# Later and fewer early weight sums, gate rows at a set place, output projection by token halves of two steps at a time

## The chip, the cores and the metric

The kernel runs on one core of a Trainium2 chip. The metric is the device time of one execution in microseconds; the time of a version is the median of several executions. The core's engines work side by side, each through its own instructions in order: TensorE (PE: matmuls and transposes), VectorE (DVE), ScalarE (ACT), GpSimd (POOL), and SyncE (SP), which here issues nearly all transfers between HBM and the on-chip memory.

## The reference

One layer of a residual block over 512 tokens of width 2048, all in float32, with 16 heads of width 128 in two groups: 8 stick-breaking heads and 8 forgetting heads, then a multilayer perceptron of hidden width 8192.

```python
h = rmsnorm(x, g_attn[l])
proj = jnp.einsum('bsd,de->bse', h, w_in[l])     # qa ka va | qf kf vf | f
...
z = z + c[:, :, i * Q_BLOCK:end, None] - c[:, :, None, :end]   # forgetting heads, c = cumsum(log_f)
p = jax.nn.softmax(jnp.where(causal, z, -jnp.inf), axis=-1)
...
a = jnp.where(causal, jnp.exp(log_beta + rest), 0.0)           # stick-breaking heads
...
x = x + concat(headnorm(oa), headnorm(ob)) @ W_out
x = x + relu(RMSNorm(x) @ W_up)^2 @ W_down
y = RMSNorm(x)
```

## The kernel before

**Numbers.** Every float32 operand is split into a high part (a cast by ACT, line 63) and a low part (a subtraction by DVE, line 64). A product is three matmuls, high x high, low x high and high x low (`mm3`, lines 95 to 98). So each block of weights costs a load on SP, a cast on ACT, a subtraction on DVE and then matmuls. Buffers for the parts come in a ring of three (`hi_lo`).

**Stages, in us of the profiled execution.** 0 to 50: x is transposed, and the first values and the gate columns f are projected (tiles accv, accm). 50 to 636: for each of 16 heads q and k are projected (`project_q`, tile accq, two steps of 24 matmuls each), the values in four groups, and the heads are worked off. 636 to 825: output projection (`out_product`, tile acco) in four column blocks n, residual and transposes. 825 to 1460: up projection. 1460 to 2050: down projection (tile accd), then the last rows.

**The attention's order on PE.** From line 529 on PE's order is written by hand: `in_turn` yields after small groups of projection matmuls, each with its time at 0.2267 us a matmul, and a table puts the heads' parts between them. Head i is at `HEAD_AT[i]`: scores there, transposes of the weights 22 us later (TURN), the product with the values 6 us after that (WEIGH, tile o), and `SUM` us after that ssq, the sum of squares for the head's norm (lines 315, 316). One PSUM bank (tag "o") holds cps, cT, ck, o and ssq in turn. DVE, ACT and SP are ordered by the scheduler.

**The gate rows.** The cumulative log gates are formed by matmuls with a triangle (cps, line 463), brought to a high and a low part on DVE (cq, chl, lines 466 to 469), transposed by four PE transposes (cT, line 472) and copied (ckT, line 474). For each forgetting head a matmul with a selector, ck (line 346), spreads one row. Before, cps and cT stand outside of the hand-written order.

**Early sums.** The up projection works unit by unit, 32 units of 256 columns, each as a 2 x 2 block product by seven products instead of eight (Strassen in Winograd's form). Three of the seven need a sum of weight blocks: t1 = b12 - b11, t3 = b22 - b12 and t2 = b22 - t1. They are formed ahead of time, during the attention, by `up_sums` (lines 156 to 164): three loads of 512 KB, three subtractions of 128x1024 on DVE, and one store to the DRAM tile td. `drip` (line 169) sets the place: behind the n-th low part of a projection step, DVE's subtractions of unit number 32 n / 62 follow. In the up projection `Unit` (line 625) loads t1, t2, t3 from td, and b21 and b22 from w_up. Products run in the order 1, 4 (of the unit before), 5, 6, 3 (of the unit before), 2, 7; product 6 takes t2. Its PSUM tiles are psa, psb and psc.

**Output projection.** `out_product` (line 228) takes two heads' rows per step: a load of w_out, its split, the split of two mixed rows (four sets of u tiles), then for each of four token blocks t two `mm3`, six matmuls. Each token block has a PSUM bank of the pool acc, which the values used before: `take_v` (line 244) splits them out of the banks into vh and vl. For n == 0 the generator runs inside the hand-written order, between the last heads' parts.

Of the kernel before, what the change touches and what calls it, by code (L numbers as in the profile page):

```python
# [14 lines left out]
P = 128  # L15
# [4 lines left out]
NH = 8  # L20
# [8 lines left out]
HEAD_AT = [26, 60, 96, 134, 163, 195, 230, 265, 294, 327, 362, 395.5, 419, 444, 468, 495]  # L29
TURN, WEIGH, SUM, VALUES_END = 22, 6, 5, 503  # L30
# [8 lines left out]
def block_kernel(ctx, tc, x, g_attn, w_in, b_f, g_out_sb, g_out_fox, w_out, g_mlp, w_up, w_down, g_final, y):  # L39
# [116 lines left out]
    def up_sums():  # L156
        r = load_sums(0)
        for u in range(NU):
            b11, b12, b22 = (r[:, j] for j in range(3))
            now, r = r, load_sums(u + 1) if u + 1 < NU else None  # L160
            dve.tensor_tensor(b11, b12, b11, op=ALU.subtract)
            dve.tensor_tensor(b12, b22, b12, op=ALU.subtract)
            dve.tensor_tensor(b22, b22, b11, op=ALU.subtract)
            yield sp.dma_start(td[u], now)
# [4 lines left out]
    def drip(ins):  # L169

        drops[0] += 1
        while drops[1] < min(NU, NU * drops[0] // 62):
            drops[1] += 1
            with tc.issue_after(ins.ins):
                next(sums)


    with (
# [49 lines left out]
        def out_product(n, mixed):  # L228
            ps = [acc.tile([P, NT], F32, tag="acc", name="acco") for _ in range(TB)]
            for k0 in range(0, 2 * NH, 2):  # L230
# [3 lines left out]
                for i in range(2):  # L234
                    ms.append(u_tile((k0 + i) % 4))
                    split(*ms[i], mixed[k0 // NH][:, (k0 + i) % NH, :])
                for t in range(TB):
                    ts = slice(t * P, (t + 1) * P)
                    for i in range(2):
                        mm3(ps[t], ms[i][0][:, ts], ms[i][1][:, ts], *w[i], k0 + i == 0, k0 + i == 2 * NH - 1)  # L240
                    yield 6 * 0.2267
# [200 lines left out]
        with tc.tile_pool(name="attp", bufs=1, space=PSUM) as atp:  # L442
# [27 lines left out]
            cT = atp.tile([P, NT], F32, tag="o", name="cT")  # L470
            for t in range(TB):
                pe.transpose(cT[:, t * P:(t + 1) * P], chl[:, t, :], ident)
            ckT = at.tile([P, NT], F32R, name="ckT")
            act.copy(ckT, cT)
# [37 lines left out]
            steps = []  # L512
# [9 lines left out]
            def run(i, part):  # L522
                with tc.high_priority():
                    if part < 0:
# [100 lines left out]
    class Unit:  # L625
        def __init__(self, u):
# [19 lines left out]
            for t_, j in ((t1, 0), (t2, 2), (t3, 1)):  # L646
                sp.dma_start(t_, td[u][:, j])
# [4 lines left out]
        def product(self, p):  # L652
# [5 lines left out]
            hi, lo = (w.rearrange("p (a b) -> p a b", b=P) for w in hi_lo(2 * NT))  # L658
            split(hi, lo, self.b[p])
# [317 lines left out]
```

## Time and profile before

| | us |
|---|---|
| three runs, median | 2084.97 (2084.62 to 2085.84) |
| profiled execution, whole | 2085.26 |
| its span | 2083.5 |
| PE busy in the span | 2055.4 |
| mean granted clock of PE | 0.997 |

The profile is one execution. Its page gives busy times, a chain of waits and groups of instructions; the trace behind it answers questions on single instructions. A row of a timeline reads: start, duration (both us), engine, line, operation, output<-inputs, shapes, and in brackets the idle time before it and what ended that. A row "L64 ... wl<-wraw,wh" is a low part of weights. A matmul's duration includes its way through the array; the distance between starts tells the pace. In a windows row, after the bounds, stand length, busy time and count of PE, weight loads, DVE, ACT and POOL, then the granted clock of PE (1.00 is full), the share of the DMA engines' time, and GB/s.

### The profile page before, as it was taken

To read this page: it belongs to the slowest core of one execution; us is meant where nothing else is said; L and a number is where in the kernel's file an instruction comes from. 1 tells how busy PE (TensorE), PEld (TensorE's weight loads), DVE (VectorE), ACT (ScalarE), POOL (GpSimd) and SP (SyncE) were. 2 spreads that over 40 slices of the span, in tenths; PEclk is the share of its full clock that TensorE was granted. 3 is DMA by queue.
4 is the path that set the end of the run, shared out by engine and by line. 5 is a ranking of instruction groups with operands and counts; after the bars stand their busy time and mean duration, and the time that the engine had idled before them with its cause. 6 is when DMAs were issued, how large, how long until landed. Compare 5 with 4: busy or idle time off the path is not lost.

```text
span 2083.5 us, 26844 instructions
## 1 busy us (share of the span) xinstructions
PE 2055.4 (99%) x10292; PEld 1747.1 (84%) x10292; DVE 1606.7 (77%) x1827; ACT 1070.1 (51%) x1426; POOL 57.1 (3%) x77
## 2 busy tenths in 40 slices
PE   9999999999999999999999999999999999999998
PEld 8788888888888888888888888888888888888886
DVE  6657848858776666788788788788789989888886
ACT  6344434445555555666666666666644444443433
POOL 0000000000110000000000000000000000000003
PEclk9999999999999999999999999999999999999999
DMA  7967957969972444677777777778856764764732
GB/s 238 342 203 245 329 175 242 334 181 293 329 251 74 158 133 151 203 263 255 250 266 258 245 265 257 246 265 295 304 200 229 254 236 164 270 231 139 271 113 81
DMA packets 361185, 481.06 MB, mean 231 GB/s; under 512 B 11952, under 2 KB 255712, under 8 KB 350944
## 3 DMA queue, kind: packets, MB, share of 16 engines
q1 hardware_dynamic: 360096, 477.21, 68.4%
q10 hardware_dynamic: 960, 2.13, 0.3%
q8 instruction: 81, 1.33, 0.2%
q14 instruction: 48, 0.39, 0.1%
HBM read 359.76 MB, written 119.54 MB: 230 GB/s over the span
## 4 chain that ended last, share of the span: by engine, by line
PE 90%; DMA 4%; DVE 4%; ACT 1%; issue 1%; SPq 0%; POOL 0%; DVEq 0%; ACTq 0%; POOLq 0%
PE psa L665 11%; PE accd L96 8%; PE accd L97 8%; PE accd L98 8%; PE psa L667 6%; PE psc L665 6%; PE accq L96 4%; PE accq L98 4%; PE accq L97 4%; PE psc L667 3%; PE psb L665 3%; PE acco L96 3%; PE acco L98 3%; PE acco L97 3%; PE accv L96 3%; PE accv L97 2%
## 5 line engine op out<-in xcount | busy, mean ns | idle before, releaser
L63 ACT CAST wh<-wraw 128x1024 fp32r<-128x1024 f32 (+2 forms) x133 | 135.4, 1019 | 201.0 <-PE accq L97 109.6
L63 ACT CAST wh<-wd 128x1024 fp32r<-128x1024 f32 (+1 forms) x136 | 135.1, 1000 | 182.3 <-PE accd L98 120.5
L64 DVE TENSOR_TENSOR wl<-wu,wh 128x1024 fp32r<-128x1024 f32 x166 | 201.6, 1219 | 32.0 <-ACT wh L63 18.3
L64 DVE TENSOR_TENSOR wl<-wraw,wh 128x1024 fp32r<-128x1024 f32 (+2 forms) x133 | 158.3, 1191 | 86.6 <-ACT wh L63 84.0
L63 ACT CAST wh<-wu 128x1024 fp32r<-128x1024 f32 x166 | 173.3, 1049 | 72.2 <-PE psc L665 20.5
L96 PE MATMUL accq<-hH,wh 128*128 128x512 f32 x512 | 201.8, 394 | 0.0
L98 PE MATMUL accq<-hH,wl 128*128 128x512 f32 x512 | 200.4, 392 | 0.0
L97 PE MATMUL accq<-hL,wh 128*128 128x512 f32 x512 | 200.1, 391 | 0.0
L64 DVE TENSOR_TENSOR wl<-wd,wh 128x1024 fp32r<-128x1024 f32 (+1 forms) x136 | 155.4, 1152 | 42.3 <-ACT wh L63 42.1
L96 PE MATMUL accd<-wh,uf 128*128 128x512 f32 x436 | 169.7, 389 | 0.9 <-issue 0.9
L97 PE MATMUL accd<-wl,uf 128*128 128x512 f32 x436 | 169.6, 389 | 0.0
L98 PE MATMUL accd<-wh,uf 128*128 128x512 f32 x436 | 169.6, 389 | 0.0
L63 ACT CAST wx<-wd 128x1024 fp32r<-128x1024 f32 (+1 forms) x88 | 87.6, 1000 | 122.1 <-PE accd L98 79.5
L64 DVE TENSOR_TENSOR wx<-wd,wx 128x1024 fp32r<-128x1024 f32 (+1 forms) x88 | 100.7, 1152 | 22.4 <-ACT wx L63 22.3
L98 PEld LDWEIGHTS accq<-hH,wl 128*128 128x128 f32 x512 | 96.4, 188 | 20.4
L97 PEld LDWEIGHTS accq<-hL,wh 128*128 128x128 f32 x512 | 96.7, 189 | 19.5
L96 PEld LDWEIGHTS accq<-hH,wh 128*128 128x128 f32 x512 | 96.6, 189 | 19.0
L96 PE MATMUL accd<-wx,uf 128*128 128x512 f32 x284 | 110.4, 389 | 1.2 <-ACT m L764 1.2
L97 PE MATMUL accd<-wx,uf 128*128 128x512 f32 x284 | 110.5, 389 | 0.0
L98 PE MATMUL accd<-wx,uf 128*128 128x512 f32 x284 | 110.5, 389 | 0.0
L766 DVE TENSOR_TENSOR m<-m,accd 128x1024 f32<-128x1024 f32 x84 | 102.0, 1214 | 10.8 <-PE accd L98 10.7
L665 PE MATMUL psa<-fl,wh 128*128 128x512 f32 x388 | 106.8, 391 | 1.8 <-DVE fl L64 1.8
(285 smaller groups left out, 4857.6 us busy)
## 6 DMA issues: line engine op xcount, KB each, us to landing
ufd<-st SPq DMA_DIRECT2D x98, 512.0 KB, 5.2
sums<-in_w_up_dram SPq DMA_DIRECT2D x96, 512.0 KB, 6.2
td<-sums SPq DMA_DIRECT2D x32, 1536.0 KB, 7.5
wd<-in_w_down_dram SPq DMA_DIRECT2D x48, 1024.0 KB, 6.5
wu<-td SPq DMA_DIRECT2D x95, 512.0 KB, 5.0
wraw<-in_w_in_dram SPq DMA_DIRECT2D x84, 512.0 KB, 5.8
uf<-ufd SPq DMA_DIRECT2D x42, 1024.0 KB, 6.7
wu<-in_w_up_dram SPq DMA_DIRECT2D x32, 1024.0 KB, 7.6
```

What stands on the lines that cost most here:

```text
L63: ins = casts[0] = act.copy(hi, src)
L64: lows[0] = dve.tensor_tensor(lo, src, hi.bitcast(F32), op=ALU.subtract)
L96: pe.matmul(out, sh, mh, start=first, stop=False, skip_group_check=True)
L97: pe.matmul(out, sh, ml, start=False, stop=False, skip_group_check=True)
L98: pe.matmul(out, sl, mh, start=False, stop=last, skip_group_check=True)
L665: pe.matmul(ps, hi[:, a, :], both, start=a == 0 and p in (1, 2, 5), stop=False, skip_group_check=True)
L667: pe.matmul(ps[:, :2 * P], lo[:, a, :], F[p][a // 4][:, a % 4, 0, :], start=False, stop=a == KC // 2 - 1, skip_group_check=True)
L766: dve.tensor_tensor(M[p][:, :, db, :], M[p][:, :, db, :], ps, op=ALU.add)
```

## The change

Five edits:

- `HEAD_AT[0]` goes from 26 to 33 and `HEAD_AT[1]` from 60 to 62; `SUM` from 5 to 7.
- The drip begins later: unit number 32 (n - 4) / 58 instead of 32 n / 62.
- For odd units the third sum t2 isn't formed early, and only two of three blocks are stored to and read from td. In its place `Unit.product` forms b22 - t1 ahead of the split of product 6, on DVE.
- The transposes of the gate rows and their copy become `turn_bias`, which the hand-written order calls at `HEAD_AT[0] - 9`, 24 us.
- In `out_product` with n == 0 the first two steps are held and then done together: twelve matmuls per token block instead of six, twice.

```diff
--- before.py
+++ after.py
@@ -26,8 +26,8 @@
 O1 = 6 * WSB
 NU = DFF // P // 2
 
-HEAD_AT = [26, 60, 96, 134, 163, 195, 230, 265, 294, 327, 362, 395.5, 419, 444, 468, 495]
-TURN, WEIGH, SUM, VALUES_END = 22, 6, 5, 503
+HEAD_AT = [33, 62, 96, 134, 163, 195, 230, 265, 294, 327, 362, 395.5, 419, 444, 468, 495]
+TURN, WEIGH, SUM, VALUES_END = 22, 6, 7, 503
 
 
 
@@ -160,8 +160,10 @@
             now, r = r, load_sums(u + 1) if u + 1 < NU else None
             dve.tensor_tensor(b11, b12, b11, op=ALU.subtract)
             dve.tensor_tensor(b12, b22, b12, op=ALU.subtract)
-            dve.tensor_tensor(b22, b22, b11, op=ALU.subtract)
-            yield sp.dma_start(td[u], now)
+            if u % 2 == 0:
+                dve.tensor_tensor(b22, b22, b11, op=ALU.subtract)
+            n = 2 if u % 2 else 3
+            yield sp.dma_start(td[u][:, :n], now[:, :n])
 
     sums = up_sums()
     drops = [0, 0]
@@ -169,7 +171,7 @@
     def drip(ins):
 
         drops[0] += 1
-        while drops[1] < min(NU, NU * drops[0] // 62):
+        while drops[1] < min(NU, NU * (drops[0] - 4) // 58):
             drops[1] += 1
             with tc.issue_after(ins.ins):
                 next(sums)
@@ -227,6 +229,7 @@
 
         def out_product(n, mixed):
             ps = [acc.tile([P, NT], F32, tag="acc", name="acco") for _ in range(TB)]
+            held = []
             for k0 in range(0, 2 * NH, 2):
                 e0 = order[k0]
                 w = load_w(w_out[e0 * P:(e0 + 2) * P, n * NT:(n + 1) * NT].rearrange("(a p) c -> p a c", p=P), 2, NT)
@@ -234,11 +237,15 @@
                 for i in range(2):
                     ms.append(u_tile((k0 + i) % 4))
                     split(*ms[i], mixed[k0 // NH][:, (k0 + i) % NH, :])
+                held += [(k0 + i, ms[i], w[i]) for i in range(2)]
+                if n == 0 and k0 == 0:
+                    continue
                 for t in range(TB):
                     ts = slice(t * P, (t + 1) * P)
-                    for i in range(2):
-                        mm3(ps[t], ms[i][0][:, ts], ms[i][1][:, ts], *w[i], k0 + i == 0, k0 + i == 2 * NH - 1)
-                    yield 6 * 0.2267
+                    for k, m, wk in held:
+                        mm3(ps[t], m[0][:, ts], m[1][:, ts], *wk, k == 0, k == 2 * NH - 1)
+                    yield len(held) * 3 * 0.2267
+                held = []
             return ps
 
         def take_v(ps, pairs=1):
@@ -467,11 +474,13 @@
             act.copy(cr, cq)
             dve.tensor_copy(chl[:, :, :NH], cr.bitcast(F32))
             dve.tensor_tensor(chl[:, :, NH:2 * NH], cq, cr.bitcast(F32), op=ALU.subtract)
-            cT = atp.tile([P, NT], F32, tag="o", name="cT")
-            for t in range(TB):
-                pe.transpose(cT[:, t * P:(t + 1) * P], chl[:, t, :], ident)
             ckT = at.tile([P, NT], F32R, name="ckT")
-            act.copy(ckT, cT)
+
+            def turn_bias():
+                cT = atp.tile([P, NT], F32, tag="o", name="cT")
+                for t in range(TB):
+                    pe.transpose(cT[:, t * P:(t + 1) * P], chl[:, t, :], ident)
+                act.copy(ckT, cT)
 
             U, CB = {}, {}
             late = {}
@@ -509,7 +518,7 @@
                 here = (lambda: late["mixed"][1][:, i - NH, :]) if i >= 2 * NH - 2 else None
                 return (attend_fox if h >= NH else attend_sb)(h % NH, i, here)
 
-            steps = []
+            steps = [(HEAD_AT[0] - 9, 0, -2)]
             for i in range(2 * NH):
                 a = HEAD_AT[i]
                 c = a + TURN + WEIGH if i != 2 * NH - 2 else VALUES_END + 3
@@ -521,7 +530,9 @@
 
             def run(i, part):
                 with tc.high_priority():
-                    if part < 0:
+                    if part < -1:
+                        turn_bias()
+                    elif part < 0:
                         CB[i] = bias_of(order[i] - NH)
                     else:
                         next(heads[i], None)
@@ -643,7 +654,7 @@
                 r, q = blocks(), blocks()
                 b11, t2, t1, t3 = r[:, 0], r[:, 1], q[:, 0], q[:, 1]
             sp.dma_start(b11, first[:, :, :P])
-            for t_, j in ((t1, 0), (t2, 2), (t3, 1)):
+            for t_, j in ((t1, 0), (t3, 1)) if u % 2 else ((t1, 0), (t2, 2), (t3, 1)):
                 sp.dma_start(t_, td[u][:, j])
             b21, b22 = wide(last)
             self.b = {1: b11, 5: t1, 6: t2, 2: b21, 7: t3, 3: b22, 4: b21}
@@ -656,6 +667,8 @@
                 self.pair = hidden[0]
                 self.c = hidden[0][:, self.u % 2]
             hi, lo = (w.rearrange("p (a b) -> p a b", b=P) for w in hi_lo(2 * NT))
+            if p == 6 and self.u % 2:
+                dve.tensor_tensor(self.b[6], self.b[3], self.b[5], op=ALU.subtract)
             split(hi, lo, self.b[p])
             if p == 2:
                 dve.tensor_tensor(self.b[4], self.b[2], self.b[6], op=ALU.subtract)
```

**Three places in the order: the gate rows (on DVE and on PE), the start of the output projection, an odd unit.** Names: wl, a low part of weights; ul, a low part of q or k; sums, the early sums; qf, a scaled q or k. First DVE, at the gate rows, before:

```order
L263 TENSOR_TENSOR qf<-accq,rb 128x512
L64 TENSOR_TENSOR wl<-wraw,wh 128x1024
L64 TENSOR_TENSOR ul<-qf,uh 128x512
L466 TENSOR_TENSOR cq<-cq,cps 128x32
L161 TENSOR_TENSOR sums<-sums 128x1024
L468 COPY chl<-cr 128x4x8
L469 TENSOR_TENSOR chl<-cq,cr 128x4x8
L162 TENSOR_TENSOR sums<-sums 128x1024
L163 TENSOR_TENSOR sums<-sums 128x1024
```

and after the change:

```order
L162 TENSOR_TENSOR sums<-sums 128x1024
L164 TENSOR_TENSOR sums<-sums 128x1024
L473 TENSOR_TENSOR cq<-cq,cps 128x32
L270 TENSOR_TENSOR qf<-accq,rb 128x512
L64 TENSOR_TENSOR wl<-wraw,wh 128x1024
L475 COPY chl<-cr 128x4x8
L476 TENSOR_TENSOR chl<-cq,cr 128x4x8
L64 TENSOR_TENSOR ul<-qf,uh 128x512
L64 TENSOR_TENSOR wl<-wraw,wh 128x1024
L161 TENSOR_TENSOR sums<-sums 128x1024
```

Before, a sum (line 161) stood between cq and chl's two rows. Now the sums of one unit end ahead of cq; behind cq come one qf and one wl, then chl, and the next unit's sums follow later.

PE at the same place, before (accq are the projection's matmuls):

```order
L463 MATMUL cps<-lf,utri 128x16
L463 MATMUL cps<-lf,onesr 128x16 x3
L463 MATMUL cps<-lf,utri 128x16
L472 MATMUL cT<-ident,chl 128x128 x4
L346 MATMUL ck<-ckT,nsel 128x512
L96 MATMUL accq<-hH,wh 128x512
L97 MATMUL accq<-hL,wh 128x512
L98 MATMUL accq<-hH,wl 128x512
```

and after, first the end of cps:

```order
L470 MATMUL cps<-lf,utri 128x16
L470 MATMUL cps<-lf,onesr 128x16 x3
L470 MATMUL cps<-lf,utri 128x16
L98 MATMUL accq<-hH,wl 128x512
L96 MATMUL accq<-hH,wh 128x512
```

and 12 accq rows later, cT:

```order
L97 MATMUL accq<-hL,wh 128x512
L98 MATMUL accq<-hH,wl 128x512
L482 MATMUL cT<-ident,chl 128x128 x4
L96 MATMUL accq<-hH,wh 128x512
L97 MATMUL accq<-hL,wh 128x512
L98 MATMUL accq<-hH,wl 128x512
```

cT followed cps directly. Now 16 accq stand between them, and 30 accq between cT and ck, which also followed each other.

PE at the start of the output projection, with the numbers of the buffers (acco_5324 and acco_5325 are the banks of the first two token blocks, wh_5330 and wl_5331 the first head row's weights of step one), before:

```order
L96 MATMUL acco_5324<-wh_5330,uh_5334 128x512
L97 MATMUL acco_5324<-wl_5331,uh_5334 128x512
L98 MATMUL acco_5324<-wh_5330,ul_5335 128x512
L96 MATMUL acco_5324<-wh_5330,uh_5338 128x512
L97 MATMUL acco_5324<-wl_5331,uh_5338 128x512
L98 MATMUL acco_5324<-wh_5330,ul_5339 128x512
L96 MATMUL acco_5325<-wh_5330,uh_5334 128x512
L97 MATMUL acco_5325<-wl_5331,uh_5334 128x512
L98 MATMUL acco_5325<-wh_5330,ul_5335 128x512
```

and after (acco_5308 is the first token block's bank, wh_5314 the first step's weights, wh_5328 the second step's):

```order
L96 MATMUL acco_5308<-wh_5314,uh_5322 128x512
L97 MATMUL acco_5308<-wl_5315,uh_5322 128x512
L98 MATMUL acco_5308<-wh_5314,ul_5323 128x512
L96 MATMUL acco_5308<-wh_5328,uh_5332 128x512
L97 MATMUL acco_5308<-wl_5329,uh_5332 128x512
L98 MATMUL acco_5308<-wh_5328,ul_5333 128x512
L96 MATMUL acco_5308<-wh_5328,uh_5336 128x512
L97 MATMUL acco_5308<-wl_5329,uh_5336 128x512
L98 MATMUL acco_5308<-wh_5328,ul_5337 128x512
L96 MATMUL acco_5309<-wh_5314,uh_5318 128x512
L97 MATMUL acco_5309<-wl_5315,uh_5318 128x512
```

The second token block followed after six matmuls; now the first block goes on through the second step's two rows, and the second block begins after twelve.

DVE in an odd unit of the up projection, after (s and c belong to the products before):

```order
L64 TENSOR_TENSOR wx<-wu,wx 128x1024
L674 TENSOR_TENSOR wu<-wu 128x8x128
L671 TENSOR_TENSOR wu<-wu 128x1024
L64 TENSOR_TENSOR wl<-wu,wh 128x1024
L703 TENSOR_TENSOR s_8624<-s_8624,psc 128x512
L64 TENSOR_TENSOR wl<-wu,wh 128x1024
L691 TENSOR_TENSOR c<-s_8624 128x256
```

The row of line 671 is the new subtraction (t2 = b22 - t1); the split of product 6 (wl) follows it.

## The prediction

> **What bounds the kernel now.** The page's first part, busy time of each engine, comes first.
>
> ```profile
> PE 2055.4 (99%) x10292; PEld 1747.1 (84%) x10292; DVE 1606.7 (77%) x1827; ACT 1070.1 (51%) x1426; POOL 57.1 (3%) x77
> ```
>
> TensorE (PE) is busy for 2055.4 of a span of 2083.5 us, so all its idle time is 28.1 us, and no change that leaves its matmuls as they are (this one does) can take more than that and what a lowered clock costs. What matters is each place where PE stands still. The view of PE's waits lists them: engine, line and tile, what was waited for, then total us, times, longest.
>
> ```profile
> PE cT L472 <- DVE chl L469: 3.3, 1, 3.3
> PE trg L380 <- POOL chl L447: 3.3, 1, 3.3
> PE acco L96 <- DVE vl L67: 2.5, 1, 2.5
> PE ssq L316 <- DVE pl L64: 2.4, 2, 1.3
> ...
> PE accd L96 <- ACT m L764: 1.2, 1, 1.2
> ...
> PE ck L346 <- ACT ckT L474: 0.7, 1, 0.7
> ```
>
> Four rows are touched: cT with ck (the gate rows), acco (start of the output projection), ssq (head norms). The trg wait is the program's start, the accd wait is in the down projection; no edited line causes them.
>
> **Part A, the gate rows.** PE's timeline around the wait, and the clock there:
>
> ```profile
> 53.41 0.60 PE L123 MATMUL trb<-ident,rw 128*128 128x128 f32 x4
> 53.76 0.48 PE L96 MATMUL accq<-hH,wh 128*128 128x512 f32 x1
> ...
> 60.70 0.39 PE L96 MATMUL accq<-hH,wh 128*128 128x512 f32 x1
> ...
> 61.83 0.40 PE L98 MATMUL accq<-hH,wl 128*128 128x512 f32 x1
> 62.07 0.17 PE L463 MATMUL cps<-lf,utri 128*128 128x16 f32 x1
> ...
> 62.98 0.26 PE L463 MATMUL cps<-lf,utri 128*128 128x16 f32 x1
> 66.59 1.08 PE L472 MATMUL cT<-ident,chl 128*128 128x128 f32 x4 [3.35 <-DVE chl L469]
> 68.35 0.80 PE L346 MATMUL ck<-ckT,nsel 128*128 128x512 f32 x1 [0.67 <-ACT ckT L474]
> 68.94 0.63 PE L96 MATMUL accq<-hH,wh 128*128 128x512 f32 x1
> ...
> 72.20 0.40 PE L98 MATMUL accq<-hH,wl 128*128 128x512 f32 x1
> ```
>
> ```profile
> 65.00:70.00 5.00, 2.74 (x8) 2.09 (x9) 3.86 (x5) 1.17 (x2) 0.00 (x0) 0.52 1.12 413
> ```
>
> In the windows row the columns behind the five engines are the granted clock (0.52), the DMA share (1.12) and GB/s. PE ends cps at 63.24, stands 3.35 us, and then runs at half clock: from 68.94 to 72.20 it issues 8 accq matmuls, 0.41 us each, where five before the wait (60.70 to 61.83) came every 0.226. From 63.24 to 72.20 are 8.96 us. The work in it is worth, at full clock, 0.35 for four transposes (trb, 53.41 to 53.76) and 9 x 0.226 for ck and eight accq: 2.39. So 6.57 us are lost: 3.35 and 0.67 waiting, 2.55 to the clock. That is the most that this edit can bring.
>
> Why 3.35? DVE, in order:
>
> ```profile
> 60.90 0.69 DVE L263 TENSOR_TENSOR qf<-accq,rb 128x512 f32<-128x512 f32 x1 [1.54 <-PE accq L98]
> 61.76 1.23 DVE L64 TENSOR_TENSOR wl<-wraw,wh 128x1024 fp32r<-128x1024 f32 x1 [0.17 <-ACT wh L63]
> ...
> 63.55 0.19 DVE L466 TENSOR_TENSOR cq<-cq,cps 128x32 f32<-128x32 f32 x1
> 65.03 1.23 DVE L161 TENSOR_TENSOR sums<-sums 128x1024 f32<-128x1024 f32 x1 [1.29 <-DMA sums<-in_w_up_dram]
> ...
> 66.26 0.18 DVE L469 TENSOR_TENSOR chl<-cq,cr 128x32 f32<-128x32 f32 x1
> ```
>
> chl's two short instructions stand behind an early sum that waits 1.29 us for its load and then takes 1.23. In the new order no sum stands between cq and chl; cps has gone 12 matmuls nearer to trb (24 accq between them, not 36, while trb itself has two accq more ahead of it), 16 accq stand between cps and cT, 30 between cT and ck. PE's times by the rows above: trb at 53.86, cps from 59.6 to 60.8 (24 x 0.226, and 1.17 for cps itself), cT at 64.4. What chl stands behind is then a qf and a wl. They wait for PE's end of a projection step, four matmuls behind cps, near 61.7; before, that end lay at 60.7, qf began 0.2 later and wl 1.06 later, so wl ends at 61.7 + 1.06 + 1.23 = 64.0 and chl near 64.3. cT and chl nearly tie: a wait of 0 to 0.1. I bound it by one more sum that slips ahead, 1.2 us, and that is no clock matter. The copy of cT has 30 matmuls, 6.8 us, of cover, against the 0.67 that ck waited behind it. I take **6.5** of 6.57; bounds 5.3 and 6.57. The moved heads themselves (33 and 62 for 26 and 60) issue what they issued; 29 us lie between them where 34 did, and later heads stand 23.5 to 38 apart without a wait, so this is costed at nothing.
>
> One rule bears on this. The Trainium skill, "TensorE: Matmul & The Clock Gate", section "Part 1: The HAM clock gate (the "warmup" mystery)", has the array fall to half clock after an idle window of about 3.4 us that runs freely, so that where a gap falls in it decides. The trace agrees as far as it goes (3.35 us idle, then 0.52), and the acco wait of 2.54 us below left the clock at 1.00. By that rule a rest of a wait would cost itself alone, and the drop might be missing in some executions, which is the fourth rival.
>
> **Part B, ssq two microseconds later in PE's order.**
>
> ```profile
> 544.64 2.96 DVE L337 TENSOR_TENSOR_SCAN w<-w 128x256 f32<-128x256 f32 x4
> ...
> 547.52 0.66 DVE L64 TENSOR_TENSOR pl<-ph,pl 128x512 fp32r<-128x512 f32 x1
> ...
> 548.24 0.50 PE L316 MATMUL ssq<-pl,onesr 128*128 128x512 f32 x1 [1.30 <-DVE pl L64]
> ...
> 608.98 0.50 PE L316 MATMUL ssq<-pl,onesr 128*128 128x512 f32 x1 [1.10 <-DVE pl L64]
> ```
>
> ssq's second matmul waits for the low part pl, and on DVE that stands behind the scans of another head (544.64 to 547.60); at 605 us it is the same. SUM from 5 to 7 puts six more 512-wide matmuls (6 x 0.226 = 1.36 us) ahead of the first and more ahead of the second. Both exceed the waits of 1.30 and 1.10: **2.4** saved, nothing added, since ssq's result goes only into the finished head. A loss is hardly possible: ssq shares one PSUM bank (tag "o") with ck and the next head's o, and these come 10 us or more after it in the table. If DVE stood later by as much, the saving would be 0; bounds 0 and 2.4.
>
> **Part C, the output projection's first two steps.**
>
> ```profile
> 636.74 0.40 PE L96 MATMUL acco<-wh,uh 128*128 128x512 f32 x1
> ...
> 640.62 0.39 PE L98 MATMUL acco<-wh,ul 128*128 128x512 f32 x1
> 643.55 0.50 PE L96 MATMUL acco<-wh,uh 128*128 128x512 f32 x1 [2.54 <-DVE vl L67]
> ```
>
> ```profile
> 637.33 1.22 DVE L64 TENSOR_TENSOR wl<-wraw,wh 128x1024 fp32r<-128x1024 f32 x1
> ...
> 643.05 0.45 DVE L67 SCALAR_TENSOR_TENSOR vl<-accv,r1v,vh 128x256 fp32r<-128x256 f32 x1
> ```
>
> ```profile
> 640.00:645.00 5.00, 2.46 (x11) 1.74 (x10) 4.92 (x7) 0.62 (x1) 0.00 (x0) 1.00 0.44 137
> ```
>
> The fourth token block needs a PSUM bank that the values' last split (vl, to 643.50) still reads. Before, PE came to it after 18 matmuls, at 641.0, and stood until 643.55, 6.8 us from the start of the stage (636.74). With both steps held, each block does 12 matmuls, so 36 stand ahead of the fourth bank, 8.1 us without counting a head's matmuls placed among them: the wait goes. The same edit makes PE want the second step's low weights after 7 matmuls, 1.6 us from the start, and wl ends at 638.55, 1.8 from it: a new wait of about 0.25. What waits behind it on PE is everything. I take **2.3**; bounds 2.54 and, if wl slips by one more DVE instruction of 1.2 us, 1.1.
>
> **Part D, odd units.** Grouped rows: the third sum (line 163), its stores and reads, and the casts' waits.
>
> ```profile
> L163 DVE TENSOR_TENSOR sums<-sums x32: 1207/1217/1532, 45.2 to 587.6; 128x1024 f32<-128x1024 f32 x32
> td<-sums SPq DMA_DIRECT2D x32, 1536.0 KB, 7.5
> wu<-td SPq DMA_DIRECT2D x95, 512.0 KB, 5.0
> L63 ACT CAST wh<-wraw 128x1024 fp32r<-128x1024 f32 (+2 forms) x133 | 135.4, 1019 | 201.0 <-PE accq L97 109.6
> ```
>
> 16 of the 32 third sums, 16 x 1.217 = 19.5 us of DVE, leave the attention and come back in the up projection; 16 stores and 16 reads of 512 KB go. In the attention nothing is won on the path: its casts mostly wait for PE to give a buffer free (109.6 of 201.0 us), so weights were ahead already. In the up projection the new subtraction stands ahead of product 6's split. There:
>
> ```profile
> 850.00:1450.00 600.00, 600.00 (x3440) 528.29 (x3439) 487.36 (x624) 389.48 (x504) 0.00 (x0) 1.00 0.75 253
> 1040.51 1.23 DVE L64 TENSOR_TENSOR wl<-wu,wh 128x1024 fp32r<-128x1024 f32 x1 [1.76 <-ACT wh L63]
> 1051.99 0.64 PE L667 MATMUL psa<-fh,wl 128*128 128x256 f32 x4
> ```
>
> PE is busy 600.00 of 600 us, DVE 487 (81%, 84% with the additions). For product 6 of unit 11, matched by tile names and bank, the low part ends at 1041.7 and PE takes it at 1052.0: 10 us ahead. 1.22 us off that is hidden. Even if my matching is one product off, the lead is over 7. I cost D at **0**; uncovered, each odd unit costs 1.22.
>
> **The sum.** 6.5 + 2.4 + 2.3 = 11.2. From the profiled execution, 2083.5 of span and 1.76 outside, 2085.26: 2074.06. It lies 0.3 above the median of the runs (2084.97), too little to matter: **2074.0**.
>
> **Rivals.**
> 1. *Slower: the subtractions come out on PE.* If DVE in the up projection had less than 1.22 us in hand, each odd unit would push its product 6: 16 x 1.22 = 19.5, less 11.2: 2093.5. It decides once the lead falls under 1.22. For it: 81% busy, and an engine that works in order; against it: 10 us of lead and not one wait of PE in 600 us. 0.07.
> 2. *The weights of the early projections come late.* PE is 6.5 us earlier from 66 on, while DMA is full (1.12) and SP issues weights behind the sums' loads. If loads don't come earlier too, A is given back: 2074.0 + 6.5 = 2080.5, and somewhat above with the waits it brings: I count it as no change. For it: the full DMA; against it: casts that wait for PE, not for DMA. 0.10.
> 3. *A wait replaces a wait.* chl behind wl by one more instruction (+1.2: 2075.2), or the second output step's weights (+1.2: 2075.2), or the edits of C don't do what they say and the bank is late all the same (+2.3: 2076.3). 0.17.
> 4. *The half clock is not in the runs that are timed.* Then A is worth 3.35 + 0.67 = 4.0, not 6.5: 2076.5. Against it: three runs within 1.2 us of each other and a profile 0.3 from their median, where the drop is 2.55. The free-running window of the page named under A would allow it. 0.04.
> 5. *New small waits* where stages meet: the first two units, whose splits are the newest, or the down projection's start, 1.2 to 5 us: 2075.2 to 2079. 0.07.
>
> **How the numbers follow.** Forecast 0.55 (2072 to 2075), rivals as said. A measurement of this kernel tells 0.2%, 4.2 us, from no change: faster is below 2080.8. The forecast and rivals 3, 4 and 5 lie there: faster 0.83; rival 2 is same 0.10; rival 1 is slower 0.07. The range starts with all bounds at their best (6.57 + 2.4 + 2.54 = 11.5) and the accd wait of 1.2 gone with the new alignment of the stages, from the fastest run, 2084.62: 2071.9. At their worst the terms leave 5.3 + 0 + 1.1 = 6.4, 2078.9; the range ends at 2080.8, so that rival 2 is half in it.
>
> **What would show it.** In the changed profile the waits of cT, ck, acco by vl and ssq are gone or below 0.3 us; the clock in 60 to 75 us is 1.00; the step at 638 us shows a wait near 0.25 for wl; psa has no wait for DVE after 850 us. Wrong would be a new row of over 1 us for accq before 110 us (rival 2), or psa rows on a subtraction (rival 1).

## The result, and the profile after

| | before | changed kernel |
|---|---|---|
| median of the runs, us | 2085.4 (2084.62 to 2086.95, 4 runs) | 2103.94 (2102.38 to 2106.97, 4 runs) |
| ratio to before | | 1.009, 95% interval 1.0072 to 1.0107 |
| profiled execution | 2085.26 | 2103.3 |
| its span | 2083.5 | 2101.5 |

The change makes the kernel 18.5 us slower. The forecast was 2074.0, 11 us faster, with a range to 2080.8. The page's first part of the changed kernel, its chain of waits by engine, and PE's waits:

```profile
PE 2063.8 (98%) x10292; PEld 1753.2 (83%) x10292; DVE 1606.8 (76%) x1827; ACT 1064.9 (51%) x1426; POOL 64.9 (3%) x77
...
PE 81%; DMA 8%; DVE 5%; ACT 3%; issue 2%; SPq 0%; DVEq 0%; ACTq 0%
```

```profile
PE psa L678 <- ACT s L684: 15.3, 11, 3.4
...
PE s L96 <- DVE pl L64: 3.1, 1, 3.1
...
PE accd L96 <- DVE c L701: 1.7, 1, 1.7
```

The waits of cT, ck, acco and ssq are gone, all four. Two others have come: 15.3 us in which a product of the up projection waits for ACT's copy (s) of what stands in its PSUM bank, and 3.1 us at a head's scores. The chain shows DMA at 8% where it had 4%.

Where the time went is seen by setting the starts of the stages side by side. From PE's timeline of before, the first product of the up projection and the first of the down projection:

```profile
826.73 1.17 PE L665 MATMUL psa<-fh,wh 128*128 128x512 f32 x4
...
1459.60 0.40 PE L96 MATMUL accd<-wh,uf 128*128 128x512 f32 x1
```

and of the changed kernel:

```profile
819.48 1.17 PE L678 MATMUL psa<-fh,wh 128*128 128x512 f32 x4
...
1478.48 0.50 PE L96 MATMUL accd<-wh,uf 128*128 128x512 f32 x1 [1.68 <-DVE c L701]
```

Everything ahead of the up projection is 7.25 us earlier. The up projection itself takes 659.00 us and took 632.87: 26.13 lost. The rest is 0.89 shorter. -7.25 + 26.13 - 0.89 = 18.0, the difference of the spans. Windows of the changed kernel (PE is the second number, the clock is third from the end):

```profile
850.00:1450.00 600.00, 584.70 (x3298) 512.11 (x3297) 483.11 (x609) 368.97 (x482) 0.00 (x0) 0.99 0.69 229
60.00:70.00 10.00, 10.00 (x52) 8.43 (x51) 5.80 (x9) 3.52 (x6) 0.00 (x0) 1.00 0.81 268
...
530.00:535.00 5.00, 5.00 (x20) 4.52 (x19) 1.87 (x2) 1.56 (x2) 0.00 (x0) 0.66 1.02 385
640.00:645.00 5.00, 5.00 (x24) 4.10 (x23) 1.81 (x4) 4.72 (x7) 0.77 (x2) 1.00 0.20 79
```

PE stands 15.3 us in the 600 us in which it had not stood at all; the first of the repaired places runs at full clock, and at 530 us there is a new stretch of half clock.

**What happens in the up projection.** The view of the new line (671), of DVE around unit 11's subtraction:

```profile
L671 DVE TENSOR_TENSOR wu<-wu x16: 1220/1226/1228, 836.8 to 1442.3; 128x1024 f32<-128x1024 f32 x16
...
  DMA wu<-in_w_up_dram: 57.8, 15
```

```profile
1029.42 1.23 DVE L674 TENSOR_TENSOR wu<-wu 128x1024 f32<-128x1024 f32 x1
1032.94 1.23 DVE L671 TENSOR_TENSOR wu<-wu 128x1024 f32<-128x1024 f32 x1 [2.29 <-DMA wu<-in_w_up_dram]
...
1039.43 1.22 DVE L64 TENSOR_TENSOR wl<-wu,wh 128x1024 fp32r<-128x1024 f32 x1
```

The last row is the split of product 6. The subtraction needs b22, and 15 of 16 times DVE stands for the load of it, 57.8 us in all. For the scheduler placed it well ahead of product 6's split. In the order of DVE's instructions with the numbers of the buffers (unit 3; wu_7417 holds b11 and t2, wu_7418 t1 and t3, wu_7422 b21 and b22):

```
L671 TENSOR_TENSOR wu_7417<-wu_7422,wu_7418 128x1024
L64 TENSOR_TENSOR wl_7428<-wu_7417,wh_7427 128x1024
L703 TENSOR_TENSOR s6_7174<-s6_7174,psc_7089 128x512
L64 TENSOR_TENSOR wl_7454<-wu_7252,wh_7453 128x1024
...
L64 TENSOR_TENSOR wx_7475<-wu_7418,wx_7475 128x1024
...
L64 TENSOR_TENSOR wl_7500<-wu_7417,wh_7499 128x1024
```

The row behind line 671 is the split of product 1 (b11); then come those of product 4 (an older unit's tile) and 5 (t1), and only the last is product 6's. So the subtraction is three splits early: 6.5 us in the rows of unit 11 above (1032.94 to 1039.43).

How that reaches PE is seen at 1229 us in the changed kernel, ACT, DVE and PE in turn:

```profile
1220.77 1.06 ACT L705 ACTIVATE c<-c 128x1024 f32<-128x1024 f32 x1 [1.57 <-DVE c L691]
1225.90 0.62 ACT L63 CAST st<-c 128x512 fp32r<-128x512 f32 x1 [4.07 <-DMA ufd<-st]
1226.43 1.04 ACT L63 CAST wx<-wu 128x1024 fp32r<-128x1024 f32 x1
1227.37 1.05 ACT L706 ACTIVATE c<-c 128x1024 f32<-128x1024 f32 x1
1228.33 0.56 ACT L684 COPY s<-psa 128x512 f32<-128x512 f32 x1
```

```profile
1226.55 0.69 DVE L64 TENSOR_TENSOR st<-c,st 128x512 fp32r<-128x512 f32 x1 [3.75 <-ACT st L63]
```

```profile
1224.88 0.64 PE L680 MATMUL psc<-fl,wl 128*128 128x256 f32 x4
1228.95 1.44 PE L678 MATMUL psa<-fh,wh 128*128 128x512 f32 x4 [3.43 <-ACT s L684]
```

ACT stands 4.07 us for a store of the hidden layer's forms (ufd) to land, because st has only three buffers; and behind this cast, in ACT's queue, waits the copy that frees the bank for product 4. The same place (unit 19) in the kernel before:

```profile
1217.41 0.62 ACT L63 CAST st<-c 128x512 fp32r<-128x512 f32 x1 [1.61 <-DMA ufd<-st]
1217.93 1.05 ACT L63 CAST wx<-wu 128x1024 fp32r<-128x1024 f32 x1
1218.89 0.57 ACT L671 COPY s<-psa 128x512 f32<-128x512 f32 x1
```

There the copy ended at 1219.46 and PE began product 4 at 1220.43: 0.97 us to spare. In the changed kernel PE could have gone on at 1225.52, and the copy ended 3.4 us later. Three things make up this difference of 4.4 us. st's low part, behind which the store is issued, ended 9.8 us ahead of the moment when PE could go on, and 10.3 before: 0.5. The store took 10.1 us from issue to landing, and 7.2 before: 2.9. And one more activation (the row at 1227.37) stands between the cast and the copy: 1.0. SP's rows with the store, in the changed kernel and then before:

```profile
1214.01 0.38 SPq L646 DMA_DIRECT2D wu<-in_w_up_dram  x1
1215.15 0.38 SPq L656 DMA_DIRECT2D wu<-in_w_up_dram  x1
1215.75 12.03 SPq L713 DMA_DIRECT2D ufd<-st  x4
```

```profile
1210.18 9.12 SPq L700 DMA_DIRECT2D ufd<-st  x4
```

So at this place a slower store weighs more than DVE's lateness. At the five longest of PE's waits (12.3 of the 15.3 us) the store took 9.3 to 10.6 us, and 6.7 to 7.8 in the same units before. Two loads stand 1.1 us apart just ahead of it (4.4 us apart before); that they slow it is not shown by a run. Two shorter waits (1.6 us together) have no store in them: there ACT's activation waits for DVE's sum c.

Over all odd units of before this lead (end of product 7's copy to the start of product 4) has a median of 1.16 us; in the changed kernel it is 0.05, which is "PE was waiting".

**What happens at 530 us.** DVE, then PE:

```profile
526.98 1.23 DVE L161 TENSOR_TENSOR sums<-sums 128x1024 f32<-128x1024 f32 x1 [1.16 <-DMA sums<-in_w_up_dram]
528.12 1.48 DVE L64 TENSOR_TENSOR pl<-pt,ph 128x1280 fp32r<-128x1280 f32 x1
```

```profile
529.66 0.53 PE L96 MATMUL s<-uh 128*128 128x512 f32 x1 [3.09 <-DVE pl L64]
```

An early sum waits for its load, the split of a head's weights stands behind it, and PE needs the bank that this split reads. It is the same figure as at 66 us before: an in-order engine with a transfer's wait at its head.

### The profile page after: what moved, and what is told of

It reads as the page before. It is cut to its first block, busy times and chain, and to the rows that moved or that the text cites. A ratio compares the mean times of both kernels' runs of the same rounds, so it can differ in the third digit from the quotient of the medians.

```text
span 2101.5 us, 26836 instructions
## 1 busy us (share of the span) xinstructions
PE 2063.8 (98%) x10292; PEld 1753.2 (83%) x10292; DVE 1606.8 (76%) x1827; ACT 1064.9 (51%) x1426; POOL 64.9 (3%) x77
## 4 chain that ended last, share of the span: by engine, by line
PE 81%; DMA 8%; DVE 5%; ACT 3%; issue 2%; SPq 0%; DVEq 0%; ACTq 0%
PE accd L96 8%; PE accd L98 8%; PE accd L97 8%; PE psa L678 7%; DMA ufd<-st 5%; PE accq L96 5%; PE accq L98 5%; PE accq L97 5%; PE psa L680 3%; PE psc L678 3%; PE acco L97 3%; PE acco L98 3%; PE acco L96 3%; PE accv L96 3%; PE accv L97 3%; PE accv L98 3%
## 5 line engine op out<-in xcount | busy, mean ns | idle before, releaser
L63 ACT CAST wh<-wu 128x1024 fp32r<-128x1024 f32 x166 | 172.1, 1047 | 46.1 <-issue 18.5
L678 PE MATMUL psa<-fh,wh 128*128 128x512 f32 x388 | 107.5, 399 | 14.2 <-ACT s L684 14.2
L64 DVE TENSOR_TENSOR wx<-wd,wx 128x1024 fp32r<-128x1024 f32 (+1 forms) x88 | 100.9, 1154 | 22.5 <-ACT wx L63 22.4
```

Of the source, the lines that this page charges most:

```text
L63: ins = casts[0] = act.copy(hi, src)
L64: lows[0] = dve.tensor_tensor(lo, src, hi.bitcast(F32), op=ALU.subtract)
L678: pe.matmul(ps, hi[:, a, :], both, start=a == 0 and p in (1, 2, 5), stop=False, skip_group_check=True)
```

## The experiments

"Stage" is the time from the first psa to the first accd in the profile (before 632.9, changed 659.0). Each time is a median beside runs of the kernel before on the same chip; these had medians of 2085.05 to 2086.24.

| run | stage | time | ratio to before, 95% interval |
|---|---|---|---|
| e1 all sums early | 633.5 | 2078.31 | 0.9959 (0.9944 to 0.9973) |
| e2 subtraction held | 635.8 | 2079.33 | 0.9968 (0.9956 to 0.9980) |
| e3 subtraction without b22 | 648.3 | 2092.31 | 1.0032 (1.0019 to 1.0045) |
| e4 wide load first | 636.1 | 2083.02 | 0.9991 (0.9982 to 1.0000) |
| e5 early place, operand there | 644.1 | 2088.55 | 1.0007 (0.9997 to 1.0016) |
| e6 held, twice | 664.1 | 2108.72 | 1.0105 (1.0090 to 1.0120) |
| e7 SUM alone | 633.1 | 2084.67 | 0.9991 (0.9982 to 1.0000) |
| e8 output projection alone | 633.9 | 2083.07 | 0.9984 (0.9974 to 0.9993) |
| e9 gate rows alone | 633.0 | 2086.00 | 1.0001 (0.9992 to 1.0010) |
| e10 gate rows, later sums | 632.7 | 2084.77 | 0.9999 (0.9989 to 1.0008) |
| e11 other source of stores | 633.5 | 2173.79 | 1.0420 (1.0405 to 1.0436) |
| e12 all but odd units and later sums | 634.5 | 2079.57 | 0.9974 (0.9964 to 0.9984) |
| e13 other source, stores in place | 632.6 | 2088.97 | 1.0019 (1.0010 to 1.0029) |
| e14 all early, old pace | 632.9 | 2076.21 | 0.9955 (0.9940 to 0.9970) |
| e15 held, old pace | 635.4 | 2076.19 | 0.9958 (0.9944 to 0.9973) |
| e16 odd units alone | 660.8 | 2111.46 | 1.0123 (1.0108 to 1.0139) |

### Is it the odd units?

e1 undoes their edit in the changed kernel, e16 makes it alone in the kernel before.

> The changed kernel with the edit on odd units undone: all three sums are formed early again and stored and read. In the changed kernel the time from the first psa to the first accd grew from 732.9 to 759.0 us (26.1); everything ahead of it is 7.25 us earlier than before. Theory 1 (the new subtraction waits for a load and holds DVE's queue): that stage is back at 732.9 +- 2, and the time is 2103.9 - 26 = 2078, 7 us below the kernel before. Rival (the later, denser attention or the new alignment of the stages costs the up projection its time, not the subtraction): the stage stays above 750 and the time above 2095.

> The kernel before with the odd-unit edit alone (third sum late, two of three blocks stored and read). If it costs what the changed kernel's stage shows, independent of the other edits: stage 632.9 + 26 = 659, time 2085.3 + 26 = 2111, less up to 3 for a lighter attention. If the cost needs the other edits (another alignment): below 2100.

(732.9 and 759.0 in the first are slips for 632.9 and 659.0.) Both came as the first theory had it: 2078.31 with the stage at 633.5, and 2111.46 with the stage at 660.8. PE's waits of e16:

```profile
PE psa L669 <- ACT s L675: 17.4, 11, 3.3
```

The same wait without any of the other edits. The odd-unit edit costs 26 us, whatever stands beside it. e1's runs spread from 2074.43 to 2081.73; the profiled one (2080.62) has a wait of 3.8 us at ssq, at 547 us.

### Is it the place, the load or DVE's time?

e2 holds the subtraction back, e3 gives it another operand, e4 moves the load of b21 and b22, e5 keeps the early place with an operand that is there, e6 is e2 with the work done twice.

```diff
 e2             if p == 6 and self.u % 2:
+                with tc.issue_after(lows[0].ins):
                     dve.tensor_tensor(self.b[6], self.b[3], self.b[5], op=ALU.subtract)
 e3
-                dve.tensor_tensor(self.b[6], self.b[3], self.b[5], op=ALU.subtract)
+                dve.tensor_tensor(self.b[6], self.b[1], self.b[5], op=ALU.subtract)
 e4 (in Unit, odd units)
+            if u % 2:
+                b21, b22 = wide(last)
             sp.dma_start(b11, first[:, :, :P])
 e5
+                with tc.issue_after(past[-4].ins):
+                    dve.tensor_tensor(self.b[6], self.b[1], self.b[1], op=ALU.subtract)
 e6
                 with tc.issue_after(lows[0].ins):
+                    for _ in range(2):
                         dve.tensor_tensor(self.b[6], self.b[3], self.b[5], op=ALU.subtract)
```

> The changed kernel with the new subtraction held on DVE behind the low part of product 5, so that it stands directly ahead of product 6's split and not three splits (some 8 us) ahead of it. The same instructions, the same loads. Theory 1a (the place in DVE's order makes the wait for the load of b22): DVE's waits at line 671 fall from 57.8 us to under 10, PE's wait for s falls from 15.3 to under 3, time 2078 +- 3. Rival (DVE has no room for 16 subtractions more, wherever they stand): 2095 or more, with PE waiting for s or for low parts.

> The changed kernel with b11 in place of b22 as the operand of the new subtraction: the same time of DVE, but an operand whose load is issued as the first of its unit. t2 of odd units is then not the reference's. Theory 1 (the wait for the load, not the 1.22 us): the waits of line 671 fall to under 10 us and the time to 2078 +- 3, though the scheduler still puts the instruction four splits ahead. Rival (DVE's time): 2095 or more.

> The changed kernel with the load of b21 and b22 issued first in odd units, ahead of b11, t1 and t3. Its median from issue to landing is 8 us, and three loads of 512 KB stand ahead of it in the changed kernel. Theory 1: if the load's place in the queue sets the wait, b22 lands some 2 to 4 us earlier, half or more of the 57.8 us of waiting goes, time 2080 to 2092; if the buffer that the load needs comes free too late, nothing changes (2104). Rival (DVE's time): 2104.

> The changed kernel with the new subtraction pinned on DVE three to four splits ahead of product 6's split, where the scheduler had it, but with b11 as both operands, which the unit's first product has read long before. t2 of odd units is then not the reference's. (In the earlier expectations the stage from the first psa to the first accd was given as 732.9 and 759.0 us; 632.9 and 659.0 are right.) Theory 1 (only the wait for a load counts): no waits at the subtraction, stage 633 to 637, time 2079 +- 2, as with the subtraction held. Rival (the place counts by itself: 1.22 us more ahead of the short sums for which ACT waits): 2088 to 2093, as with b11 and t1.

> The changed kernel with the new subtraction held directly ahead of product 6's split and issued twice, so 16 x 1.22 = 19.5 us of DVE more than in the held version (2079.3, stage 635.8). Theory (DVE has room there, as the prediction had it): within 3 us of it, 2077 to 2083. Rival (DVE's room was just used up): 2090 or more, up to 2079.3 + 19.5 = 2099.

e2 came as expected: 2079.33, and PE's waits for s are 2.0 us. ScalarE's wait for the stores, 38.1 us in 850 to 1450 before and 55.5 in the changed kernel, is now

```profile
ACT st L63 <- DMA ufd<-st: 7.5, 8, 2.3
```

e4 came inside its bounds, 2083.02: the stage is 636.1, and the subtraction waits 28.5 us, now for t1. e3 and e5 missed. Theory 1 wanted 2078 and 2079, its rivals 2095 or more and 2088 to 2093. e3 gave 2092.31 with 13.8 us of waits for t1; e5, where the subtraction waits for nothing, gave 2088.55, its rival's value. Its rows, ACT first, then PE:

```profile
ACT st L63 <- DMA ufd<-st: 70.9, 30, 6.4
```

```profile
PE psa L682 <- ACT s L688: 8.4, 8, 2.2
```

So the wait for b22 is only part of it: 659.0 to 644.1 of the stage, 15 us. The other 8, down to 635.8, stay when the subtraction stands early and finds its data ready. What is left there is 1.22 us of DVE's work ahead of the short work that ACT's queue needs: the lead of product 7's copy has a median of 0.08 us, and the stores whose landing the casts ahead of it wait for took 8.0 to 10.4 us in the odd units 7 to 29 (6.5 to 8.6 before). ACT's total of waits for the stores doesn't price this: 38.1 us cost nothing before, 55.5 went with 26 us in the changed kernel, 70.9 with 11 in e5. The versions also differ in how the scheduler lays the rest, so this split into 15 and 8 is rough.

e6 missed outright: 2108.72 where the prediction's view of DVE, "room there", wanted 2077 to 2083. PE's waits of e6:

```profile
PE psa L680 <- ACT wh L63: 19.4, 9, 2.6
```

Now the weights' casts come late, 19.4 us of waiting: the cast of product 6 cannot begin until the held subtraction has run, and ACT's queue stands behind it. In e2 the smaller of the two leads of product 6 in odd units, cast to high product and low part to low product, has a median of 3.4 us; before it was 9.7. Holding costs 6 us of lead and doubling 3 more: in e6 the median is 0.4, and at every second odd unit it is 0.1 at most. That DVE is busy 81 or 84% of the time said nothing of this.

### On which way does it reach PE?

e11 and e13 leave every cast and subtraction as in the changed kernel, but the form stores send a part of the F tiles, so that st's buffers never wait for a store to land. In e13 each store still waits for st's low part and stands where it stood.

```diff
-            sp.dma_start(ufd[g0][p][:, :, j0:j0 + 2, :], st.bitcast(F32))
+            go = sp.dma_start(ufd[g0][p][:, :, j0:j0 + 2, :], F[1][0][:, 0:2].bitcast(F32))
+            tc.add_manual_dep(go.ins, lows[0].ins.name, ...)
```

> The changed kernel, but the stores of the up projection's forms (ufd) send a part of the F tiles in place of st: the same transfers and the same casts and subtractions, only the three buffers of st no longer wait for a store to land, and the stores no longer for st's low part. The hidden layer that the down projection reads is then not the reference's. In the changed kernel ScalarE waits 59.9 us for those stores ahead of st's cast, and the copy of psa that TensorE waits for stands behind it in the same queue. Theory 2 (VectorE's delay at the new subtraction reaches TensorE through st's buffers and ScalarE's queue): PE's waits for s fall from 15.3 to under 4, the stage from 659.0 to under 642, the time below 2086. Rival (the delay reaches PE on other ways as well, through the sums that Relu waits for or late low parts): 2092 or more.

> The changed kernel with a part of the F tiles as the source of the form stores in place of st, each store made to wait for st's low part as before: every transfer stays at its place in the queue, but st's buffers are free without a store's landing. The hidden layer that the down projection reads is then not the reference's. Theory 2 (the delay reaches TensorE through st's three buffers and ScalarE's queue): the waits at the new subtraction stay above 30 us, ScalarE's waits for the stores are gone, the stage from the first psa to the first accd is under 642 us (changed kernel 659.0), the time under 2087. Rival (traffic or the other ways): the stage stays above 650, the time above 2095.

In e11 the stores, bound to nothing, slipped into the output projection and starved its weights (PE waited 81.9 us there): 2173.79, no use as a time. Its stage is 633.5, but with the stores' traffic gone from it. e13 settles it. DVE's waits and PE's waits in the stage:

```profile
DVE wu L671 <- DMA wu<-in_w_up_dram: 43.4, 15, 5.5
```

```profile
PE psa L678 <- ACT s L684: 2.7, 1, 2.7
PE psa L678 <- DVE fl L64: 1.8, 1, 1.8
```

DVE still stands 43.4 us at the subtraction, the stores go where they went, ScalarE has no wait for a store left, and the stage is 632.6. Like for like it is 636.6: 18 matmuls of the down projection (tile m, 4.1 us at 0.2267) lie inside this stretch in the other runs and behind its end in e13. That is 22.4 us under the changed kernel and 3.8 over before. So st's three buffers with ACT's queue behind them are the way for 22 of the 26 us. The whole time, 2088.97, missed the expected 2087: the start of the down projection takes 5.8 us more than before there, with 4.4 us of waits for the splits of weights and a stretch of half clock; why was not followed up.

### The other three edits, and 530 us

e7, e8 and e9 are one edit each in the kernel before, e10 is e9 with the later sums, e12 the changed kernel without odd units and later sums.

```diff
 e7
-TURN, WEIGH, SUM, VALUES_END = 22, 6, 5, 503
+TURN, WEIGH, SUM, VALUES_END = 22, 6, 7, 503
 e10 (e9 without this line; e12 with the old line)
-        while drops[1] < min(NU, NU * drops[0] // 62):
+        while drops[1] < min(NU, NU * (drops[0] - 4) // 58):
 e14, e15
+        while drops[1] < min(NU, drops[0] - 5, NU * drops[0] // 62):
```

> The kernel before with SUM 7 for 5 and nothing else. The prediction's part B: the two ssq waits (2.4 us) go and nothing comes: 2083. In the changed kernel those waits are gone, but a new wait of 3.1 us stands at a head's scores (529.66 us, for the split of pt behind an early sum that waits for its load). If SUM makes that wait, it is here too, and the time is 2085 to 2087; if the other edits make it, it isn't.

> The kernel before with the output projection's first two steps by halves and nothing else. The prediction's part C: the acco wait of 2.54 us goes, a wait of up to 0.25 us for the second step's low weights comes, 2.3 us less: 2083.1. In the changed kernel the time from the first acco to the first psa fell from 189.99 to 187.57 us; the same is expected here: 187.6 +- 0.3.

> The kernel before with the gate rows' transposes at their set place and heads 0 and 1 moved, and nothing else (the early sums begin as before). If the set place alone does part A: cT's wait and the half clock go, the first accq after 75 us is 6 us earlier, time 2085.4 - 6.3 = 2079. If the later sums are needed for it (a sum stands ahead of chl again), a wait of 1 to 3 us stays at cT and the time is 2080 to 2084.

> As the run of the gate rows alone, and with the later start of the early sums. Part A as predicted: 2079. In the changed kernel a wait of 3.1 us and 1.2 us of half clock came at a head's scores at 530 us, behind an early sum whose load was late; if the later start of the sums (or the earlier TensorE) makes that, it is here too, and the time is 2082 to 2084; if SUM makes it, it isn't.

> The changed kernel with all three sums early again and the sums begun as before: the gate rows, SUM and the output projection's halves remain. Sum of the parts as they were measured, 6.3 + 2.4 + 2.4 = 11.1: 2074.3, if nothing new comes at the scores; 2078 (as with the later start) if the wait at the scores comes from TensorE being earlier in a part where the transfers are full.

e8 did what was expected: 2083.07, and first acco to first psa 187.5 us (635.19 to 822.72). e7 removed the two ssq waits, 2.4 us, and a wait of 1.0 us at the scores came: 2084.67, by its interval between 0 and 0.2% faster. Its output projection begins 2.7 us earlier than before and its up projection only 1.2, since the acco wait of 2.5 us, which it keeps, is followed by half clock here (last section). e9 missed: with its transposes at the set place alone, cT still waits 3.3 us and the clock drops behind it. DVE there shows why:

```profile
64.75 1.23 DVE L161 TENSOR_TENSOR sums<-sums 128x1024 f32<-128x1024 f32 x1 [1.13 <-DMA sums<-in_w_up_dram]
65.90 0.18 DVE L466 TENSOR_TENSOR cq<-cq,cps 128x32 f32<-128x32 f32 x1
66.50 1.23 DVE L162 TENSOR_TENSOR sums<-sums 128x1024 f32<-128x1024 f32 x1 [0.43 <-DMA sums<-in_w_up_dram]
...
67.73 0.18 DVE L469 TENSOR_TENSOR chl<-cq,cr 128x32 f32<-128x32 f32 x1
```

Two sums with waits stand ahead of chl. It takes both edits together. e12, which has the old beginning of the sums, keeps a cT wait of 2.9 us for that reason: 2079.57, not the 2074.3 that the sum of the parts gave. In e10, with both, the projections after the gate rows run 7.1 us earlier than before; a wait of 1.1 us at 193 us takes 1.4 of them back, the stretch around 530 us with a wait at the scores (2.6 us) 4 more, and by the output projection 1.0 is left. So SUM does not make that wait; the later sums do, or PE's being earlier. e14 and e15 part the two.

> The changed kernel with all three sums early, and the early sums begun at the sixth step but back on the old pace from the tenth step on. If the denser pace makes the wait at 530 us: no wait for s or ssq above 1.5 us there, the first acco at 627 to 629 us, time 2085.3 - 6.3 - 2.4 - 2.4 = 2074. If TensorE's being 6 us earlier in a full stretch of transfers makes it: as the run with all sums early, 2078.

> The same pace of the early sums, with the odd units' third sum formed late but held directly ahead of product 6's split. One third sum in two and a sixth of the sums' traffic less in the attention, 1 to 3 us more in the up projection: 2075 if the pace makes the wait at 530 us, 2079 if not.

Begun late but on the old pace from the tenth step on, the sums leave 530 us alone. PE's waits of e14 in 515 to 560 us hold one row:

```profile
528.84 0.50 PE L96 MATMUL s<-uh 128*128 128x512 f32 x1 [1.05 <-DVE pl L64]
```

e15 has none there. The first acco comes at 629.8 and 629.0 us, a little later than expected, and the times are 2076.21 and 2076.19, the best of all. Both beat the kernel before and the changed one. e14's time lies between the two that its expectation named, 2074 and 2078, since one sum stands ahead of chl again, with 0.8 us of wait at cT, and 1.1 us of wait stayed at the scores. Ahead of 530 us PE is 5 us earlier than before in both, so the pace makes the wait there and not PE's being earlier; that the pace acts through the sums' loads is read from the trace of the changed kernel, not from a run of its own.

## Why the prediction was wrong

- **Part A was right in mechanism and size.** cT at 64.80 (forecast 64.4) with no wait, the clock 1.00, and the projections from 170 to 525 us 6.3 us earlier than before, where 6.5 was forecast. It rested on no sum standing between cq and chl, which by e9 takes the later start of the sums; that the denser pace behind this start has a price later was not said.
- **Part B was right for ssq and missed what replaced it.** The 2.4 us of waits went. The new wait at the scores is neither in the sum nor among the rivals; rival 2 named the full transfers but put them on the projections' weights before 110 us, where nothing happened. With the half clock behind it the wait took 4.5 us: the projections' lead over the kernel before falls from 6.35 to 1.81 us across it.
- **Part C was right.** First acco to first psa fell by 2.4 us (2.3 forecast); the 0.25 us for the second step's low weights did not show. A, B and C left 7.25 us ahead of the up projection, not 11.2.
- **Part D is where it failed**, at "I cost D at 0". Three things in that step did not hold. The row of DVE's order behind the new subtraction was taken for product 6's split; it is product 1's, and the subtraction stands three splits earlier. So its operand, which would have been there at the split (in the kernel before b22 of unit 11 landed 6 us ahead of that split), is not there. And the cover was measured at the wrong place: "10 us ahead" is the lead of the weights' low part over PE, but DVE's delay goes to PE by st's three buffers, ACT's queue and the PSUM bank, and there the lead had a median of 1.16 us in odd units. Nor does the cover named stay when the subtraction stands at the split: product 6's lead falls from 9.7 to 3.4 us (e2), to 0.4 with one subtraction more, and then 28 us are lost (e6).
- **Rival 1** had the sign, the engine and the condition (a lead under 1.22), at 0.07 and with a price of 19.5. It asked for the lead of the split too, and priced DVE's time alone. The loss is 26.1: 16.7 us of new waits on PE in the stage (15.3 of them for s), 6.8 us for four stretches of 3.41 us at half clock behind them, and 2.6 us that the rows don't give.
- The sentence "not one wait of PE in 600 us" was true and no evidence. A lead of 0.05 us (the least in before) and one of 10 us look the same in a list of waits.

## What to carry to other kernels

Before an instruction is added to an in-order engine, look up the place that the scheduler gives it, by buffer and not by row, and whether its operand has landed there; then price the wait, not the duration. The cover is the smallest lead on any way from that engine to the bounding one, ring buffers and PSUM banks included, and a list without waits does not give it. Work that depends on a load should stand directly ahead of its user, and work that was moved out of one full stretch lands in another: change its beginning without changing its pace.

## What the runs showed of the hardware

PE's clock falls after shorter rests than the 3.35 us of the gate rows. In e6 the same wait of 2.44 us was followed by half clock at one place and by full clock at another. Timeline and windows of e6 (in the first row four matmuls take 2.07 us, in the second 1.20):

```profile
968.52 2.07 PE L680 MATMUL psa<-fh,wh 128*128 128x512 f32 x4 [2.44 <-ACT wh L63]
...
1050.97 1.20 PE L680 MATMUL psa<-fh,wh 128*128 128x512 f32 x4 [2.44 <-ACT wh L63]
```

```profile
968.00:972.00 4.00, 3.48 (x9) 2.76 (x10) 4.00 (x6) 2.36 (x3) 0.00 (x0) 0.57 0.81 227
...
1050.00:1054.00 4.00, 3.03 (x13) 2.51 (x14) 4.00 (x7) 3.63 (x4) 0.00 (x0) 1.00 0.74 210
```

The clock in the traces tells the two apart. From 75 us on, the stretches of half clock within one trace begin whole multiples of 3.41 us apart (in the changed kernel's up projection at 984.0, 1065.9, 1229.7 and 1393.6 us: 24, 48 and 48 steps) and last one such step or several. What differs is how much rest falls into one step: of e6's two waits 2.3 us lay in the step ahead of 968.4, but only 1.8 in the step ahead of 1050.3. The acco wait of 2.54 us lay in two steps in the kernel before, 1.0 and 1.5 us, and the clock stayed at 1.00; in e7 the same wait lay in one step, and the next step ran at half clock:

```profile
637.70:641.00 3.30, 0.76 (x4) 0.34 (x3) 3.30 (x6) 0.00 (x0) 0.00 (x0) 1.00 0.34 127
641.10:644.40 3.30, 3.30 (x9) 2.55 (x9) 2.29 (x3) 1.78 (x3) 0.00 (x0) 0.50 0.47 159
```

In all traces, between 75 and 2060 us, half clock followed every step with 1.90 us of rest or more and never began behind a step with less than 1.68; between the two it came at some places and not at others. So a wait of 2.4 us may cost half clock or not.

The Trainium skill ("TensorE: Matmul & The Clock Gate", "Part 1: The HAM clock gate (the "warmup" mystery)") gives about 3.4 us of a freely running idle window. The free run and the step of 3.41 us agree with these traces; that the window must be idle does not, since 1.90 us of rest in it were enough.
